# Full 128-row operands on TensorE: zero-filled low keys, padded edge tiles, and rows of rstd by transposition

## The chip, the cores and the metric

One core of a Trainium2 chip (trn2) runs the whole program in one launch. The metric is the device time of that launch in microseconds, the median of several runs. A "row" of TensorE below is a row of the contraction: the partitions over which a matmul sums. The profile writes a matmul's shape as rows\*columns of the stationary operand, then rows x columns of the moving one, so `64*128 64x256` sums over 64 partitions and moves 256 columns.

## The reference, cut to what matters

Two transformer blocks follow each other on 512 tokens of 1024 features, in float32, each of two layers. Attention heads have 64 dimensions, so a product of queries and keys sums over 64 numbers.

```
# block 1, each layer: gated MLP, three kinds of attention side by side, gated MLP
x = x + 0.5 * swiglu(rmsnorm(x), ...)
out_a = sliding_window_attn(8 heads, 2 key heads, window 128, sinks, T5 bias)
out_b = moba_attn(4 heads)             # causal softmax attention
out_c = dsa_attn(4 heads, one shared key head, the 128 best keys of each query)
x = x + concat(out_a, out_b, out_c) @ w_out
x = x + 0.5 * swiglu(rmsnorm(x), ...)
# block 2, layer 0 (even): 512 latent and 256 context tokens
q, k = rms_norm(q over 64, gain), rms_norm(k over 64, gain)    # of every head
o_a = window_attention(8 heads, latent window + context)        # with rope
o_b = neighbourhood_attention(8 heads, 8 rows x 16 columns of the grid + context)
# block 2, layer 1 (odd): latent attention, 16 heads of 64 + 32 dimensions
# both layers: residuals with gates, then a squared-ReLU MLP
```

The products run in a reduced float32 format (F32R); for accuracy each operand is split into a high part and a low part (value minus high part), and three of the four cross products are summed.

## The kernel before, in words

`Net.build` emits block 1 (`block1`: `ffn`, `mixer1`, `ffn`, twice) and block 2 (`even_mixer`, MLP, `odd_mixer`, MLP). Weights are loaded in 512 KB pieces by SP, split by ScalarE (`whi`) and VectorE (`wlo`, helper `weights`, L145 to L154), and multiplied on TensorE (`mm`, L133; `mm3`, L136). Nearly all matmuls therefore stand on L134, and VectorE's subtractions of a high part on L143 (`lo`). The framework sets an instruction order on each engine by the program's order and its own estimates; the kernel interleaves streams by generators (`weave`, `slots`, `pipeline`), so that projections or output products stand between the steps of attention. Each engine works its list in order. PSUM banks are named rings: in the attention stages "mm" has 3 banks, "s" (scores) 2, "pt" (transposed probabilities) 2, "o" 1.

**Scores of block 1** (`mixer1`). A head's query tile holds its high part on 64 partitions and its low part on the other 64; the key tile `a` holds the high part of the keys twice. One 128-row product gives high x high plus low x high. The third term, high x low, is a second product on 64 rows: the low keys of two heads lie on the two halves of one tile `l`, and `dot` (L552) multiplies the slice `half(e)` of queries and of `l`. `keys` (L532) makes these tiles: four copies on ScalarE and one subtraction on VectorE. Heads A and B take this form: per layer 4 tiles of queries x 8 heads, and 4 x 4, 48 products on 64 rows. Heads C share one key head that stands on both halves (`shared`), and take 128 rows in both products.

**Neighbourhood heads of block 2** (heads B of `even_mixer`, L1342 on). `prepare(h)` makes `qs` (queries, high and low), `ks` (keys, high twice) and `kl`, whose low part fills 64 partitions only. `attend(h, t)` has three stages, skewed by a unit each: `s1` scores (`dot`), bias and minimum on VectorE, exponential on ScalarE; `s2` transposes the probabilities to `pt`, copied to `ptb`; `s3` multiplies with the values `vb`. The tiles 0 and 3 see 192 latent keys, cut as 64 + 128, so one of their blocks has 64 rows. There are 8 heads x 6 tiles; tiles 0 to 3 have two `dot` calls, tiles 4 and 5 one: 80 in all, each of one product on 128 and one on 64 rows.

**Rows of rstd.** A norm over features sums over partitions, so its result comes with tokens on partitions and must become a row. Two helpers do that. `rstd_rows` (L203) spreads a column over 128 columns and multiplies it with the identity in float32, one product for each 128 tokens; 68 such columns in the program. `head_rows` (L1028), for two heads at once, transposes four columns (high and low of both, made by two small operations of VectorE in `head_stats`) to a tile `rows` of 4 partitions, copied by ScalarE; then a product with the constant `c_E` spreads these 4 rows to 128 partitions. It serves 13 chunks of queries and keys in `even_mixer` (`qk`: stages `evac`, `stats`, `rows`, `final`, `rotate`), the denominators of heads A (`finish_a`), the rope keys and the denominators of `odd_mixer` (`finish`): 44 products on 4 rows. For heads B the latent tokens are kept column by column of the grid (`colmajor`), and 8 of these products read `rows` in that order.

Of the kernel before, what the change touches and what calls it, by code (L numbers as in the profile page):

```python
# [17 lines left out]
T = 512  # L18
# [15 lines left out]
# column offsets of the packed per-feature vectors  # L34
# [15 lines left out]
for _n, _w in (("cos", 512), ("sin", 512), ("perm", 128), ("J", 128), ("mask_a", 640), ("mask_b", 640), ("E", 128),  # L50
               ("ones", 8), ("rt", 256), ("kr", 768), ("m2", 128)):
    CCOL[_n] = (NCST, _w)
    NCST += _w


def constants():
    """Tables that depend on shapes alone."""
# [35 lines left out]
    put("E", (np.arange(4)[:, None] % 2 == (p // 64)[None, :]).astype(np.float32))  # L93
# [9 lines left out]
    # of each token tile: cosines, then sines as they stand before the rotation of the keys' dimensions  # L103
# [10 lines left out]
class Stream:  # L114
    """tokens [c0, c0 + m) of a residual tile [128, 8, ..] and the modulation that they take"""
# [10 lines left out]
class Net:  # L126
# [51 lines left out]
    def rsqrt(self, y, v, w):  # L178
        """y = v ** -0.5 on a small tile, in float32; w is scratch of y's shape."""
# [11 lines left out]
    def rstd_y(self, acc, nt, dim, tag="mm"):  # L191
        """acc [128, nt*128]: partial sums of squares over partitions.  Returns y [128 token, nt]."""
# [27 lines left out]
    def consts(self, es):  # L220
# [5 lines left out]
        # the table of functions is loaded while the first operands come in  # L226
# [5 lines left out]
        self.c_E = cp.tile([4, 128], F32R, name="E4")  # L232
        with tc.tile_pool(name="set", bufs=1, side="right", reuse_waits="tile") as sp:
# [4 lines left out]
            nc.vector.tensor_copy(self.c_E, self.cst("E", sp, rows=4))  # L238
# [3 lines left out]
    def bias_tables(self):  # L242
        """T5 biases of heads A (window) and B, C (causal) as [query, head, key] tiles, negated; 1e30 where masked."""
# [38 lines left out]
    def pipeline(self, units):  # L282
        """Emit the stages of each unit skewed by one step; yields after every stage."""
# [27 lines left out]
    def weave(self, main, n, fill, total):  # L311
        """Emit main (n yields) with the fill (total yields) spread evenly in between."""
# [8 lines left out]
    def push(self, d, g):  # L321
        """Split chunk d of the residual, scaled by the gain in column g, for the sublayer that follows."""
# [110 lines left out]
    def pv(self, o_ps, blocks, vs):  # L433
        """o_ps [128, 64] = sum over blocks of P^T blocks (stationary) and V blocks (moving)."""
# [3 lines left out]
    def o_norm(self, o_ps, rden, nh):  # L438
        o = self.op.tile([128, 512], F32, name="o", bufs=2)
# [5 lines left out]
    def o_out(self, o, nh, dst, cols):  # L445
        """transpose o [128, nh * 64] and split it into dst = (hi, lo) [128, nh/2, tokens]."""
# [9 lines left out]
    def mixer1(self, l, nxt):  # L456
        nc, tc = self.nc, self.tc
        win, wo = self.ins["win"], self.ins["wo"]
        with ExitStack() as es:
# [7 lines left out]
            def proj(b, dst, scale=1.0):  # L467
                """one 128-column block of h @ w_in, transposed, into the tile or function dst; yields four times."""
# [37 lines left out]
            # Of two heads e on the halves of the partitions: queries [high; low] and [low; high], keys [high; high] of  # L506
            # each and the low parts as they stand
            def half(e):
                return slice(64 * e, 64 * e + 64)
# [4 lines left out]
            def ring_k(dt=F32R):  # L514
                return new("k", T, dt=dt, bufs=10)
# [16 lines left out]
            def keys(dst):  # L532
                def f(t):
                    a, b, l = [ring_k() for _ in range(3)]
                    nc.scalar.copy(a, t)
                    self.lo(l, t, a)
# [3 lines left out]
                    dst.extend([[(a, slice(0, 128)), (l, half(0))], [(b, slice(0, 128)), (l, half(1))]])  # L540
                return f

            def shared(dst):
                """keys that all heads take, on both halves already"""
                def f(t):
# [3 lines left out]
                    dst.extend([(a, slice(0, 128)), (l, slice(0, 128))])  # L549
# [20 lines left out]
            # token-major columns: va 128, vb 256, widx 4  # L570
# [15 lines left out]
            # C selects keys: scores of the index heads, then the 128 largest of each row  # L586
# [34 lines left out]
            def attn(i, heads, ob_, nh, sink, dst):  # L621
                """units of one query tile; heads: (q, k, n, bias, selection, [v blocks], sink) in order."""
# [70 lines left out]
            # phase 1: index scores between the projections of A  # L693
# [14 lines left out]
            # phase 2: A between the projections of B  # L708
# [70 lines left out]
            def fill3():  # L779
# [11 lines left out]
                t = new("t", T, bufs=2)  # L791
# [34 lines left out]
    def adaln(self):  # L826
        """generator over (layer, 128-feature block): mod[:, layer, block, cond] = silu(cond) @ ada_w."""
# [19 lines left out]
    def finish_mod(self):  # L847
# [4 lines left out]
        # gain * (1 + scale): [128, layer, sublayer, cond, chunk]  # L852
# [9 lines left out]
    def square_acc(self, s, d):  # L862
        """s.acc += squares of chunk d"""
# [9 lines left out]
    def modulate(self, s, l, sub, ma=None):  # L873
        """s.xs: split chunks of norm(x) * (1 + scale) + shift; one chunk for each step"""
# [16 lines left out]
    def normalise(self, s, l, sub, delay, gap):  # L891
        """statistics, rows of rstd and modulation of a stream, step by step"""
# [9 lines left out]
    def lin(self, w, xss, ps):  # L902
        """ps[j] [128, m] += w @ xss[j]; one step for each chunk"""
# [8 lines left out]
    def gate(self, l, k, d, s, p):  # L912
        """chunk d of the residual += gate * p"""
# [1214 lines left out]
```

## Time and profile before

| | |
|---|---|
| median of 3 runs | 3787.88 us (3785.65 to 3790.46) |
| the profiled execution: span, first to last instruction | 3790.3 us |
| PE busy | 3710.3 us (98%), 18814 matmuls |
| VectorE, ScalarE, GpSimd busy | 2246.8, 1496.8, 150.6 us |
| mean granted clock of TensorE | 0.981 of full speed |

The span is all that the profile records of its execution; it stands 2.4 us (0.06%) over the median. A matmul's record reaches from its start to the modelled end of its pipeline, so records overlap and "busy" says little; what a matmul takes from the next one is the distance from its start to the next start. A merged line of the timeline shows the first start of several equal matmuls.

### The profile page before, as it was taken

The page shows a single profiled execution, that of the slowest core. Times are in us where ns is not written, and L with a number is a line of the kernel's source. Part 1 is how long each engine was busy: PE and PEld are TensorE (multiplying, and loading weights), DVE is VectorE, ACT ScalarE, POOL GpSimd, SP SyncE. Part 2 cuts the span into 40 slices and gives each one's busy share as a digit, 9 for nine tenths or more (in the row PEclk, how much of TensorE's full clock was granted, in tenths as well). Part 3 has the DMA queues.
Part 4 walks back from the last instruction along what each step waited for, and adds up shares of the span by engine and source line. Part 5 has one row for each costly group of instructions (what it writes and reads, how often), then busy time and mean ns, then how long its engine had stood idle before and what let it go on. Part 6 is the DMA issues. An engine that isn't in the chain of part 4 may idle for free. (4 is left out here: it accounts for less than half of the span.)

```text
span 3790.3 us, 47958 instructions
## 1 busy us (share of the span) xinstructions
PE 3710.3 (98%) x18814; PEld 3093.8 (82%) x18814; DVE 2246.8 (59%) x4205; ACT 1496.8 (39%) x2580; POOL 150.6 (4%) x150
## 2 busy tenths in 40 slices
PE   8999999999999999999999999999999989999999
PEld 6888887888888887888887887778888877888887
DVE  6576675767576657654456675463333468876443
ACT  4223554322322246442234554441221347764222
POOL 1000002000000000100000000000000100100000
PEclk9999999999999999999999998899999999999999
DMA  6454212445454432133331011022112310013332
GB/s 221 127 165 144 81 57 84 156 156 167 128 168 149 141 115 63 51 116 95 100 102 59 29 49 50 17 73 67 62 62 62 90 63 24 23 52 105 99 96 95
DMA packets 115482, 356.53 MB, mean 94 GB/s; under 512 B 12468, under 2 KB 23096, under 8 KB 114744
## 3 DMA queue, kind: packets, MB, share of 16 engines
q1 hardware_dynamic: 106432, 341.32, 28.4%
q10 hardware_dynamic: 8824, 12.15, 1.1%
q8 instruction: 147, 2.41, 0.3%
q14 instruction: 79, 0.65, 0.1%
HBM read 340.85 MB, written 12.58 MB: 93 GB/s over the span
## 5 line engine op out<-in xcount | busy, mean ns | idle before, releaser
L134 PE MATMUL mm<-xs,whi 128*128 128x512 f32 (+1 forms) x3840 | 1193.3, 392 | 15.1 <-ACT whi L150 9.0
L150 ACT CAST whi<-wraw 128x1024 fp32r<-128x1024 f32 (+3 forms) x528 | 542.1, 1028 | 1603.7 <-PE mm L134 1290.1
L134 PEld LDWEIGHTS mm<-xs,whi 128*128 128x128 f32 x3840 | 718.9, 189 | 166.7 <-ACT whi L150 11.1
L134 PE MATMUL mm<-h,whi 128*128 128x512 f32 (+1 forms) x2944 | 822.2, 372 | 2.0 <-ACT whi L150 2.0
L143 DVE TENSOR_TENSOR wlo<-wraw,whi 128x1024 fp32r<-128x1024 f32 (+3 forms) x528 | 630.4, 1194 | 309.3 <-ACT whi L150 299.5
L134 PE MATMUL mm<-xs,wlo 128*128 128x512 f32 (+1 forms) x1920 | 750.3, 391 | 5.5 <-DVE wlo L143 5.2
L134 PEld LDWEIGHTS mm<-h,whi 128*128 128x128 f32 x2944 | 536.0, 188 | 108.9 <-ACT whi L150 2.2
L134 PE MATMUL mm<-h,wlo 128*128 128x512 f32 (+1 forms) x1472 | 515.9, 372 | 1.2 <-DVE wlo L143 1.2
L134 PEld LDWEIGHTS mm<-xs,wlo 128*128 128x128 f32 x1920 | 363.4, 189 | 85.3 <-DVE wlo L143 11.0
L134 PE MATMUL mm<-xslat,whi 128*128 128x512 f32 x1024 | 344.0, 413 | 11.1 <-ACT whi L150 3.6
L134 PEld LDWEIGHTS mm<-h,wlo 128*128 128x128 f32 x1472 | 264.5, 189 | 41.4 <-DVE wlo L143 1.6
L835 DVE CUSTOM_DVE_ANT_0 junk<-wraw,silu_c 128x1024 f32<-128x1024 f32 x192 | 234.5, 1221 | 97.3 <-DMA wraw<-in_ada_w 94.6
L914 DVE SCALAR_TENSOR_TENSOR x<-mm,mod,x 128x512 f32<-128x512 f32 (+1 forms) x96 | 67.7, 706 | 295.2 <-PE mm L134 295.2
L134 PEld LDWEIGHTS mm<-xsctx,whi 128*128 128x128 f32 x944 | 175.5, 193 | 41.3 <-ACT w L1105 2.9
L134 PEld LDWEIGHTS mm<-xslat,whi 128*128 128x128 f32 x1024 | 170.1, 194 | 47.0 <-DVE xslat L888 5.4
L134 PE MATMUL mm<-xslat,wlo 128*128 128x512 f32 x512 | 208.0, 407 | 0.5 <-DVE wlo L143 0.5
L134 PE MATMUL mm<-xsctx,whi 128*128 128x256 f32 x944 | 195.1, 289 | 0.1
L343 DVE SCALAR_TENSOR_TENSOR x<-mm,x 128x512 f32<-128x512 f32 x144 | 99.2, 689 | 129.9 <-PE mm L134 129.5
L397 DVE TENSOR_TENSOR t<-mm,R 128x512 f32<-128x512 f32 x88 | 60.8, 691 | 138.6 <-PE mm L134 138.1
L395 DVE TENSOR_TENSOR t<-mm,R 128x512 f32<-128x512 f32 x88 | 60.7, 689 | 135.4 <-PE mm L134 135.4
L134 PE MATMUL mm<-xsctx,wlo 128*128 128x256 f32 x472 | 134.2, 285 | 0.0
L134 PEld LDWEIGHTS mm<-xslat,wlo 128*128 128x128 f32 x512 | 99.1, 194 | 7.5 <-DVE wlo L143 1.4
(405 smaller groups left out, 4739.2 us busy)
## 6 DMA issues: line engine op xcount, KB each, us to landing
wraw<-in_gu SPq DMA_DIRECT2D x176, 512.0 KB, 3.6
wraw<-in_mlp_w SPq DMA_DIRECT2D x136, 512.0 KB, 3.5
wraw<-in_ada_w SPq DMA_DIRECT2D x96, 512.0 KB, 3.6
wraw<-in_dn SPq DMA_DIRECT2D x64, 512.0 KB, 3.7
wraw<-in_win SPq DMA_DIRECT2D x30, 512.0 KB, 3.5
wraw<-in_dn SPq DMA_DIRECT2D x32, 384.0 KB, 3.2
wraw<-in_ewin SPq DMA_DIRECT2D x18, 512.0 KB, 3.4
wraw<-in_wo SPq DMA_DIRECT2D x16, 512.0 KB, 3.6
```

The costliest lines, as they stand in the source:

```text
L134: self.nc.tensor.matmul(ps, lhsT, rhs, start=start, stop=stop)
L143: self.nc.vector.tensor_tensor(out, x, hi.bitcast(F32), op=OP.subtract)
L150: nc.scalar.copy(hi, raw)
L343: self.nc.vector.scalar_tensor_tensor(self.x[:, d, :], ps, scale, self.x[:, d, :], op0=OP.mult, op1=OP.add)
L395: nc.vector.tensor_mul(zg, ps[0], R)
L397: nc.vector.tensor_mul(zu, ps[1], R)
L835: nc.vector.tensor_tensor_reduce(j, w, self.silu_c[:, c, :], 1.0, 0.0, op0=OP.mult, op1=OP.add, accum_out=self.mod[:, l, f, c:c + 1])
L914: self.nc.vector.scalar_tensor_tensor(s.chunk(d), p, self.mod[:, l, k + d, s.cond:s.cond + 1], s.chunk(d), op0=OP.mult, op1=OP.add)
```

## The change

All products of queries and keys take 128 rows. In `mixer1` each head gets a low tile of its own (`la`, `lb`), whose other half GpSimd sets to zero; `keys` subtracts in two halves. In `prepare`, GpSimd zeroes the other half of `kl`. In `attend` the context stands first, the latent keys behind it, and the edge tiles are padded: the last 64 columns of `s` are zeroed, and `vb` has blocks for keys 0 to 127 and 128 to 255, so every block has 128 rows. `rstd_rows` transposes the spread column and no longer multiplies. `spread` (new) copies each of two columns 64 times on ScalarE, `head_rows` transposes that tile straight to PSUM, and VectorE multiplies from there; `c_E`, the high and low columns, `rows` and the stage `rows` go. To make room, `t` in `mixer1` and the tiles `o` and `sh` have one buffer where they had two; the ring `k` has 13 where it had 10. Comments go as well.

```diff
 def rstd_rows(self, y, nt, tag="mm"):
-                self.mm(pr[:, j * 128:(j + 1) * 128], y[:, j0 + j:j0 + j + 1].to_broadcast([128, 128]), self.ident,
-                        True, True)
+                self.nc.tensor.transpose(pr[:, j * 128:(j + 1) * 128], y[:, j0 + j:j0 + j + 1].to_broadcast([128, 128]),
+                                         self.ident)
...
 # mixer1
-                t = new("t", T, bufs=2) if f else dst
+                t = new("t", T) if f else dst
...
-                return new("k", T, dt=dt, bufs=10)
+                return new("k", T, dt=dt, bufs=13)
...
 def keys(dst):
-                    a, b, l = [ring_k() for _ in range(3)]
+                    a, b, la, lb = [ring_k() for _ in range(4)]
+                    nc.gpsimd.memset(la[64:].bitcast(F32), 0.0)
+                    nc.gpsimd.memset(lb[:64].bitcast(F32), 0.0)
                     nc.scalar.copy(a, t)
-                    self.lo(l, t, a)
+                    self.lo(la[:64], t[:64], a[:64])
+                    self.lo(lb[64:], t[64:], a[64:])
...
-                    dst.extend([[(a, slice(0, 128)), (l, half(0))], [(b, slice(0, 128)), (l, half(1))]])
+                    dst.extend([(a, la), (b, lb)])
...
 def dot(o, q, k, q0, k0, k1):
-                for i, (t, r) in enumerate(k):
-                    self.mm(o, q[r, q0:q0 + 128], t[r, k0:k1], i == 0, i == len(k) - 1)
+                for i, t in enumerate(k):
+                    self.mm(o, q[:, q0:q0 + 128], t[:, k0:k1], i == 0, i == len(k) - 1)
...
 def head_stats(self, sq, ones, nt, qscale, tag="mm"):
-        ys = self.sm.tile([128, nt, 4], F32R, name="ys%d" % nt)
-        y3 = y.rearrange("p (j c) -> p j c", c=2)
-        nc.vector.tensor_scalar(ys[:, :, 0:2], y3, qscale, None, op0=OP.mult)
-        nc.vector.scalar_tensor_tensor(ys[:, :, 2:4], y3, qscale, ys[:, :, 0:2].bitcast(F32),
-                                       op0=OP.mult, op1=OP.subtract)
-        return ys
+        if qscale != 1.0:
+            nc.vector.tensor_scalar(y, y, qscale, None, op0=OP.mult)
+        return y
...
+    def spread(self, y, nt):
+        t = self.rowp.tile([128, nt * 128], F32, name="spread")
+        self.nc.scalar.copy(t.rearrange("p (c d) -> p c d", d=64), y[:, :, None].to_broadcast([128, 2 * nt, 64]))
+        return t
+    def head_rows(self, t, c0, c1, tag="mm"):
+        p = self.psum(tag)
+        for j in range(c0, c1, 128):
+            self.nc.tensor.transpose(p[:, j - c0:j - c0 + 128], t[:, j:j + 128], self.ident)
+        return p[:, :c1 - c0]
...
 # even_mixer, qk: final
-                        p = self.psum()
-                        r = st["rows"][:, c0:c1]
+                        p, d = self.head_rows(st["y"], c0, c1), st["d"][:, c0:c1]
                         if colmajor and c0 == 0:
-                            r = r.rearrange("p (r c) -> p c r", r=8)
-                            self.mm(p[:, :c1 - c0].rearrange("p (c r) -> p c r", r=8), self.c_E, r, True, True)
-                        else:
-                            self.mm(p[:, :c1 - c0], self.c_E, r, True, True)
-                        nc.vector.tensor_mul(st["d"][:, c0:c1], st["d"][:, c0:c1], p[:, :c1 - c0])
+                            d = d.rearrange("p (c r) -> p c r", r=8)
+                            p = p.rearrange("p (r c) -> p c r", r=8)
+                        nc.vector.tensor_mul(d, d, p)
...
-                return proj(b, [evac, stats, rows, final] + ([rotate, lambda st: dst(st["d"])] if keep else []))
+                return proj(b, [evac, stats, final] + ([rotate, lambda st: dst(st["d"])] if keep else []))
...
 # even_mixer, heads B
+                nc.gpsimd.memset(l[o].bitcast(F32), 0.0)
                 self.lo(l[r], kb[r, c], k[r])
...
-            values = [[(0, 64, 5), (64, 128, 0)], [(0, 128, 0), (128, 128, 1)], [(0, 128, 1), (128, 128, 2)],
-                      [(128, 64, 6), (0, 128, 2)], [], []]
+            values = [[5, 7], [0, 1], [1, 2], [2, 6], [], []]
...
-                        self.mm(o, q[half(e), t * 128:(t + 1) * 128], l[half(e), k0:k1], False, True)
+                        self.mm(o, q[:, t * 128:(t + 1) * 128], l[:, k0:k1], False, True)
+                    if nl % 128:
+                        nc.gpsimd.memset(s[:, n:], 0.0)
+                    dot(p[:, :256], T, TT)
...
 # odd_mixer
 def finish(c, job):
-                ys = new(gp, "ys", 4, 4, dt=F32R, bufs=2)
-                d3 = den.rearrange("p (i h) -> p i h", h=2)
-                nc.vector.tensor_copy(ys[:, :, 0:2], d3)
-                nc.vector.tensor_tensor(ys[:, :, 2:4], d3, ys[:, :, 0:2].bitcast(F32), op=OP.subtract)
+                rows = self.spread(den, 4)
                 yield
-                rows = self.head_rows(ys, 4)
-                yield
-                p = self.psum()
-                self.mm(p, self.c_E, rows, True, True)
-                nc.vector.tensor_mul(of[:, c, :], of[:, c, :], p)
+                nc.vector.tensor_mul(of[:, c, :], of[:, c, :], self.head_rows(rows, 0, T))
```

Because stages fall away and estimates differ, the order on the engines moves too. On TensorE, in heads B of block 2, a stretch between two output products stood so before (`ks` high keys, `kl` low keys, `pt` transposed probabilities, `o` product with the values; the size is that of the output):

```order
L1147 MATMUL pt<-ident,s 64x128
L1147 MATMUL pt<-ident,s 128x128 x3
L134 MATMUL o<-vb,ptb 128x64 x4
L134 MATMUL s<-ks,qs 128x256
L134 MATMUL s<-kl,qs 128x256
L1147 MATMUL pt<-ident,s 128x128 x2
L134 MATMUL o<-vb,ptb 128x64 x4
```

The same stretch now:

```order
L1136 MATMUL pt<-ident,s 128x128 x4
L133 MATMUL o<-vb,ptb 128x64 x4
L133 MATMUL s<-ks,qs 128x256
L133 MATMUL s<-kl,qs 128x256
L1136 MATMUL pt<-ident,s 128x128 x2
L133 MATMUL o<-vb,ptb 128x64 x4
```

The number of instructions is the same; the block of 64 keys has become one of 128, and each product on `kl` still follows its partner on `ks`.

On TensorE, in the projections of `even_mixer`, the first chunk of keys took its two 4-row products here before (`rows,E`; the six transpositions of `ys` stood some thirty products ahead):

```order
L134 MATMUL mm<-xsctx,wlo 128x256
L134 MATMUL mm<-rows,E_69 128x512
L134 MATMUL mm<-xsctx,whi 128x256 x2
L134 MATMUL mm<-xsctx,wlo 128x256
L134 MATMUL mm<-xslat,whi 128x512 x2
L134 MATMUL mm<-xsctx,whi 128x256
L134 MATMUL mm<-rows,E_69 128x256
```

In their place now:

```order
L133 MATMUL mm<-xsctx,wlo 128x256
L1032 MATMUL mm<-ident,spread 128x128 x4
L133 MATMUL mm<-xslat,whi 128x512 x2
L133 MATMUL mm<-xsctx,whi 128x256 x2
L133 MATMUL mm<-xslat,wlo 128x512
L1032 MATMUL mm<-ident,spread 128x128 x2
```

The six transpositions, of 128 columns where they had 4, have come to the place of the two products on 4 rows.

On ScalarE, in the same projections, two copies of `rows` stood between the evacuations (`kb`, `w`) and the split of the next weights before:

```order
L1037 CAST rows<-mm 4x512
L1037 CAST rows<-mm 4x256
L150 CAST whi<-wraw 128x1024
L1104 ACTIVATE kb<-mm,vecs 128x512
L1104 ACTIVATE kb<-mm,vecs 128x256
```

Now one copy, which waits for VectorE's `hy`, stands there:

```order
L1024 COPY spread<-hy 128x768
L149 CAST whi<-wraw 128x1024
L1024 COPY spread<-hy 128x768
L1099 ACTIVATE kb<-mm,vecs 128x512
L1100 ACTIVATE w_16059<-mm 128x512
```

Two copies have become one, one step earlier, ahead of TensorE's transposition instead of behind it.

## Rows read from the trace of the kernel before

**Rows 1.** The page: span, and busy time of TensorE with its share.

```profile
span 3790.3 us, 47958 instructions
PE 3710.3 (98%) x18814; PEld 3093.8 (82%) x18814; DVE 2246.8 (59%) x4205; ACT 1496.8 (39%) x2580; POOL 150.6 (4%) x150
```

**Rows 2.** Timeline of TensorE, heads B of block 2: start, us, form, count.

```profile
2332.16 0.38 PE L134 MATMUL s<-kl,qs 64*128 64x256 f32 x1
2332.47 0.38 PE L134 MATMUL s<-ks,qs 128*128 128x256 f32 x1
2332.79 0.38 PE L134 MATMUL s<-kl,qs 64*128 64x256 f32 x1
2333.10 0.66 PE L1147 MATMUL pt<-ident,s 128*128 128x128 f32 x4
2333.69 1.24 PE L134 MATMUL o<-vb,ptb 64*128 64x64 f32 x8
2334.77 0.83 PE L1147 MATMUL pt<-ident,o 128*128 128x128 f32 x6
```

**Rows 3.** Groups of TensorE by form: count, busy us, mean ns; 64-row scores.

```profile
L134 PE MATMUL s<-kl,qs 64*128 64x256 f32 x64 | 26.8, 422 | 0.0
L134 PE MATMUL s<-k,x 64*128 64x256 f32 x48 | 18.3, 382 | 0.0
...
L134 PE MATMUL s<-k,q 64*128 64x128 f32 x8 | 2.6, 323 | 0.0
```

**Rows 4.** Timeline of TensorE, projections of `even_mixer`.

```profile
2040.83 0.28 PE L134 MATMUL mm<-xsctx,wlo 128*128 128x256 f32 x1
2041.03 0.49 PE L134 MATMUL mm<-rows,E 4*128 4x512 f32 x1
2041.45 0.73 PE L134 MATMUL mm<-xslat,whi 128*128 128x512 f32 x2
2042.02 0.39 PE L134 MATMUL mm<-xsctx,whi 128*128 128x256 f32 x2
2042.25 0.40 PE L134 MATMUL mm<-xslat,wlo 128*128 128x512 f32 x1
```

**Rows 5.** Groups of TensorE by form: the 4-row products, the spread columns of rstd.

```profile
L134 PE MATMUL mm<-ident,y 128*128 128x128 f32 x120 | 18.8, 302 | 8.5 <-DVE y L186 8.5
...
L134 PE MATMUL mm<-rows,E 4*128 4x512 f32 x22 | 13.1, 597 | 0.0
```

**Rows 6.** Timeline of TensorE: four spread columns in the first MLP.

```profile
38.64 0.62 PE L134 MATMUL mm<-xs,whi 128*128 128x512 f32 x2
39.10 0.39 PE L134 MATMUL mm<-xs,wlo 128*128 128x512 f32 x1
39.32 1.05 PE L134 MATMUL mm<-ident,y 128*128 128x128 f32 x8
40.13 0.71 PE L134 MATMUL mm<-xs,whi 128*128 128x512 f32 x2
```

**Rows 7.** Windows: length, busy us (count) by engine, granted clock, DMA share, GB/s.

```profile
447.00:566.00 119.00, 118.90 (x599) 93.94 (x598) 89.97 (x280) 72.00 (x178) 0.00 (x0) 0.90 0.18 59
1430.00:1549.00 119.00, 118.71 (x596) 94.06 (x596) 89.45 (x278) 71.26 (x178) 0.00 (x0) 0.90 0.19 59
2284.00:2448.00 164.00, 163.62 (x840) 128.41 (x840) 80.97 (x240) 78.04 (x177) 0.00 (x0) 0.85 0.08 21
2018.00:2268.00 250.00, 244.92 (x1543) 201.64 (x1543) 164.85 (x468) 130.62 (x283) 0.00 (x0) 1.00 0.10 32
3140.00:3390.00 250.00, 237.47 (x1536) 206.21 (x1537) 214.84 (x431) 187.30 (x400) 22.67 (x49) 0.97 0.07 21
```

**Rows 8.** Groups by form of VectorE, GpSimd and ScalarE: nearest to what is added.

```profile
L143 DVE TENSOR_TENSOR k<-t,k 128x512 fp32r<-128x512 f32 x3 | 2.0, 681 | 0.0
...
L253 POOL MEMSET v<- 128x1024 f32 x2 | 1.9, 956 | 23.1 <-DMA scr<-v 23.1
...
L1767 ACT ACTIVATE s<-s,mx 128x768 f32<-128x768 f32 x64 | 58.1, 907 | 7.8 <-DVE mx L1766 7.4
```

More of the change, by code (lines that the diff above doesn't have):

```diff
@@ L49 @@
 NCST = 0
-for _n, _w in (("cos", 512), ("sin", 512), ("perm", 128), ("J", 128), ("mask_a", 640), ("mask_b", 640), ("E", 128),
+for _n, _w in (("cos", 512), ("sin", 512), ("perm", 128), ("J", 128), ("mask_a", 640), ("mask_b", 640),
                ("ones", 8), ("rt", 256), ("kr", 768), ("m2", 128)):
@@ L1019, in head_stats @@
         self.rsqrt(y, v, w)
-        ys = self.sm.tile([128, nt, 4], F32R, name="ys%d" % nt)
-        y3 = y.rearrange("p (j c) -> p j c", c=2)
-        nc.vector.tensor_scalar(ys[:, :, 0:2], y3, qscale, None, op0=OP.mult)
-        nc.vector.scalar_tensor_tensor(ys[:, :, 2:4], y3, qscale, ys[:, :, 0:2].bitcast(F32),
-                                       op0=OP.mult, op1=OP.subtract)
-        return ys
-    def head_rows(self, ys, nt, tag="mm"):
-        nc = self.nc
-        rows = self.rowp.tile([4, nt * 128], F32R, name="rows")
-        for j0 in range(0, nt, 4):
-            k = min(4, nt - j0)
-            pr = self.psum(tag)
-            for j in range(k):
-                nc.tensor.transpose(pr[:4, j * 128:(j + 1) * 128], ys[:, j0 + j, :].bitcast(F32), self.ident)
-            nc.scalar.copy(rows[:, j0 * 128:(j0 + k) * 128], pr[:4, :k * 128])
-        return rows
+        if qscale != 1.0:
[10 more added lines that the diff above has]
+        return p[:, :c1 - c0]
     def cst(self, name, pool, rows=128):
@@ L1108, in stats @@
                 def stats(st):
[L1109 to L1112 removed]
+                    st["y"] = self.spread(self.head_stats(st["sq"], self.c_ones[:, 0:2], 6, qscale), 6)
                 def final(st):
                     for c0, c1 in self.bands(TT):
[L1116 to L1117 removed]
+                        p, d = self.head_rows(st["y"], c0, c1), st["d"][:, c0:c1]
                         if colmajor and c0 == 0:
[L1119 to L1123 removed]
+                            d = d.rearrange("p (c r) -> p c r", r=8)
+                            p = p.rearrange("p (r c) -> p c r", r=8)
+                        nc.vector.tensor_mul(d, d, p)
                 def rotate(st):
@@ L1184, in vb_t @@
                 p = self.psum("pt")
-                tr(p[:, 0:128], t[:, 640:768])
-                tr(p[:64, 128:256], t[:, 0:64])
-                tr(p[:64, 256:384], t[:, 448:512])
-                nc.scalar.copy(vb[:, 4, c], p[:, 0:128])
-                nc.vector.tensor_copy(vb[:64, 5:7, c], p[:64, 128:384].rearrange("p (a b) -> p a b", b=128))
+                for j, s in enumerate((640, 0, 448, 128)):
+                    tr(p[:, j * 128:(j + 1) * 128], t[:, s:s + 128])
+                nc.scalar.copy(vb[:, 4:8, c], p.rearrange("p (a b) -> p a b", b=128))
             va_u = vproj(0, va_t)
@@ L1282, in finish_a @@
                 nc.vector.reciprocal(den, den)
-                ys = new(pa, "ys", 6, 4, dt=F32R, bufs=2)
-                d3 = den.rearrange("p (i h) -> p i h", h=2)
-                nc.vector.tensor_copy(ys[:, :, 0:2], d3)
-                nc.vector.tensor_tensor(ys[:, :, 2:4], d3, ys[:, :, 0:2].bitcast(F32), op=OP.subtract)
-                yield
-                rows = self.head_rows(ys, 6, "pt")
+                rows = self.spread(den, 6)
                 yield
                 for c0, c1 in self.bands(TT):
-                    p = self.psum("pt")[:, :c1 - c0]
-                    self.mm(p, self.c_E, rows[:, c0:c1], True, True)
+                    p = self.head_rows(rows, c0, c1, "pt")
                     nc.vector.tensor_mul(oa[:, c, c0:c1], oa[:, c, c0:c1], p)
-                yield
+                    yield
             def attention_a(c, after):
@@ L1433, in s2 @@
                     p = self.psum("pt")
-                    for k, (c0, w, v) in enumerate(blocks):
-                        tr(p[:w, k * 128:(k + 1) * 128], u["s"][:, c0:c0 + w])
-                    full = [k for k, b in enumerate(blocks) if b[1] == 128]
-                    f0, f1 = full[0], full[-1] + 1
-                    nc.scalar.copy(ptb[:, f0 * 128:f1 * 128], p[:, f0 * 128:f1 * 128])
-                    if f0:
-                        nc.vector.tensor_copy(ptb[:64, :128], p[:64, :128])
+                    for k in range(len(blocks)):
+                        tr(p[:, k * 128:(k + 1) * 128], u["s"][:, k * 128:(k + 1) * 128])
+                    nc.scalar.copy(ptb[:, :128 * len(blocks)], p[:, :128 * len(blocks)])
                 def s3():
@@ L1445, in s3 @@
                     o = st[e]["o"]
-                    for k, (c0, w, v) in enumerate(blocks):
-                        self.mm(o[:, t * 64:(t + 1) * 64], u["pt"][:w, k * 128:(k + 1) * 128], vb[:w, v, h * 64:h * 64 + 64],
+                    for k, v in enumerate(blocks):
+                        self.mm(o[:, t * 64:(t + 1) * 64], u["pt"][:, k * 128:(k + 1) * 128], vb[:, v, h * 64:h * 64 + 64],
                                 k == 0, k == len(blocks) - 1)
@@ L1562, in odd_mixer @@
         ykv = self.rstd_y(acc["kv"], 6, 256)
-        ykr = self.head_stats(sq, self.c_ones[:, 6:8], 6, 1.0)
+        ykr = self.spread(self.head_stats(sq, self.c_ones[:, 6:8], 6, 1.0), 6)
         evac(0, "q", proj(0, (lat,)))
@@ L1566, in odd_mixer @@
         evac(1, "q", proj(1, (lat,)))
-        rows = self.head_rows(ykr, 6)
         evac(2, "q", proj(2, (lat,)))
@@ L1709, in odd_mixer @@
         for c0, c1 in self.bands(TT):
-            p = self.psum()
-            self.mm(p[:, :c1 - c0], self.c_E, rows[:, c0:c1], True, True)
-            nc.vector.tensor_mul(t[:, c0:c1], t[:, c0:c1], p[:, :c1 - c0])
+            nc.vector.tensor_mul(t[:, c0:c1], t[:, c0:c1], self.head_rows(ykr, c0, c1))
         v = kv(0)
```

33 lines of the change are left out of this document (9 added, 24 removed).

## The prediction, made before the changed kernel was timed

> **What bounds the kernel.** I read the page first: TensorE has a matmul in flight for 3710.3 of 3790.3 us [rows 1]. The reader is to see two things: no other engine comes near, and so whatever shortens TensorE's own list shortens the kernel, as long as operands arrive in time. But "busy" is no measure of use, so the second view is the timeline of TensorE, read from start to start. Plain products set the scale: two of 256 columns take 0.23 us, 0.115 each [rows 4], two of 512 columns 0.46, 0.23 each [rows 6]. In heads B of block 2 the same 256 columns take 0.31 us, whether on 64 rows or on the 128 rows between them: starts at 2332.16, 2332.47, 2332.79, 2333.10 [rows 2]. The product on 4 rows shows where it is lost: the 256-column product ahead of it takes 0.20 and not 0.115, it takes 0.42 itself and not 0.23, and the two of 512 behind it 0.57 and not 0.46 [rows 4]. So going from 128 rows to fewer costs some 0.09 + 0.19 us, and going back 0.1, beside the products themselves: about 0.39 for a visit. The third view, windows by stage, tells what each stage could give: all engines' work, and the granted clock [rows 7].
>
> **The change, part by part.** Durations are of the profiled execution, whose span of 3790.3 us stands 2.4 us over the median of the runs.
>
> *Low products on 128 rows.* There are 176: 80 on `kl`, and 96 in block 1, which the groups by form confirm ([rows 3]: first, second and last of eight groups, 176 in all). A product gets no longer by its rows, since 0.115 is the step on 128 rows. Between two score products a visit of 0.39 us goes; where transpositions follow, the way back costs less (four take 0.59 to the next start, of which four plain ones at 0.11 are 0.44, and 0.09 is already the next visit's entry [rows 2]). I take 0.37. 176 x 0.37 = **65 us**, all on TensorE's list.
>
> *Products on 4 rows.* All 44 go, with their visits: 18 of 512 columns at 0.42 + 0.20, 18 of 256 at 0.12 + 0.39, and the 8 that read by columns of the grid: the 22 records of the group of 512 columns average 597 ns [rows 5], 14 of them last 490 [rows 4], so the 8 last 0.78, which is 0.71 from start to start, and 0.20 for the visit's ends. 11.2 + 9.2 + 7.3 = **27 us**, rounded down. The transpositions ahead of them keep their number, and 128 columns are taken at the same 0.11.
>
> *Edge tiles.* Eight passes of `o`, two of them on 64 rows, take 1.08 us [rows 2]; plain ones take 0.11 each, and 0.09 goes ahead of them. 16 x 0.27 = **4 us**.
>
> *Columns of rstd.* Four columns are eight passes, 0.81 us [rows 6]; four transpositions are 0.44. With 136 passes (120 in [rows 5], 16 more on "pt") there are 17 such fours: 17 x 0.4 = **7 us**, most of it in stages where TensorE waits for nothing.
>
> *The clock.* Three stages run at a granted clock of 0.90, 0.90 and 0.85 [rows 7]. Between the levels 1.2 and 2.4 GHz that is 20, 20 and 30% of their time at the lower one: 24 + 24 + 49 = 97 us, which at 2.4 GHz would be 48 less. Before it fell, TensorE was in exactly these visits. Bounds are 0 and 48; no row shows these stages without visits, but the window with as many transpositions and none of the 64-row products, heads A of block 2, has 1.00 [rows 7]. I take half, **24 us**, since each of these stages also begins with waits that remain.
>
> *What is given back.* In the two attention stages of block 1 TensorE would be left with 119 - 48 x 0.37 - 6 (its part of the clock) = 95 us, while VectorE has 90 us of work there [rows 7] and gets two more subtractions of 0.68 us [rows 8]. No stage here runs VectorE above 86% (214.84 of 250 [rows 7]); at 90% the stage takes 101, so 6.5 us for each: **-13 us**. Heads B come to 164 - 30 - 4 - 12 = 118 us with VectorE at 81 and ScalarE at 78: two thirds, no charge. Heads A with their projections lose some 21 of 250 and keep VectorE at 72%: none.
>
> *At nothing.* GpSimd's zeroes: 12 of 64x512, 8 of 64x768, 16 of 128x64, each under the 0.96 us of 1024 columns [rows 8]; GpSimd is idle in these stages [rows 7], and the tiles have two or more buffers, so they are written a unit ahead. If all of them were waited for, it would be some 15 us. The copy to `spread`: 768 columns, at most 0.91 us [rows 8] in place of two; behind it on ScalarE stand evacuations, for whose banks TensorE waits, but at least 4 us of products lie between the statistics and the transposition. The single buffer of `t`: the next projection's evacuation waits on VectorE for four copies on ScalarE, under 3 us, and a projection of 24 products of 0.23 lies between (5.5 us); if that cover were gone, `topk` and the scores' minimum are what queues behind it. VectorE's multiplication that reads PSUM in another order: as long as before.
>
> Sum: 65 + 27 + 4 + 7 + 24 - 13 = **114 us**. 3790.3 - 114 = 3676; against the median, **3674 us**. The whole 97 us at 2.4 GHz and nothing given back would be 151, 3637; only the first four terms, and the stages of block 1 stopped at VectorE's 80% (114 us, 13 worse each) with 12 us of zeroes waited for, 65, 3723.
>
> **A rule that speaks against it.** The rows say that a short product is paid like a visit of 0.39 us. The Trainium skill, "TensorE: Matmul & The Clock Gate", Part 3 (Packing small matmuls), holds that products on different row groups run side by side, a few ns apart, so that short ones should be kept and packed; by that rule the first term would be 0, which is rival 3 below, with its time and its chance. Here a 128-row product stands between any two short ones, and none of the starts [rows 2] are closer than 0.31 us.
>
> **Rivals.**
> 1. *The other engines become the bound.* Scores, minimum, exponential, transposition, copy and product form a chain; heads B have 48 units, and the time of one falls from 3.4 to 2.4 us. For it: VectorE at 76% in block 1 already [rows 7]. Against it: the stages are skewed by a unit. With block 1 at 110 and heads B at 130 us, and 12 more of waits in heads A, the gain is 75: 3713 us.
> 2. *The clock stays at 2.4 GHz.* For it: it falls only where the visits are densest. 24 more than the forecast and part of the 13: 3642 us.
> 3. *Filling up gains nothing.* If the low product took 0.31 us because its operands alternate with the high one's, or if short products ran beside their neighbours, the visits would not be the price, and only the 4-row products and the columns of rstd would go: 34 us, 3754. Against it: products on 4 rows with other operands show the same ends [rows 4].
> 4. *Slower: the clock falls.* Shorter products leave TensorE waiting on VectorE, and more of the 538 us (652 - 114) of these four stages runs at 1.2 GHz. A microsecond of work costs one more there; without the clock's term the gain is 90, and 48 us of work is at 1.2 GHz now, so the kernel is slower when more than 138 of the 538, a quarter, are there. With a third, 179, it is 41 slower: 3829 us. For it: the three stages that are at the lower level for up to 30%. Against it: with the visits gone the products stand closer, and heads A have 1.00 with 250 us of the same kind of work [rows 7]. The same page of the Trainium skill, Part 4 (PE-mode transpose), says that transpositions do not count as work for the clock; more products become transpositions here. By it this rival would hold, but heads A, full of transpositions, contradict it.
>
> **How the numbers follow.** Forecast 57%, rival 1 16%, rival 2 20%, rival 3 3%, rival 4 4%. A difference under 0.2% cannot be told from none here. Forecast and rivals 1 to 3 are all faster by more, 95% with 1% set aside for no change; slower is 4%. From 3632 to 3722 the range takes in the forecast with both bounds of the clock, and most of rivals 1 and 2.
>
> **What would show it.** Right: score products of 256 columns 0.12 us apart; no record with 64 or 4 rows; heads B in about 118 us, each attention stage of block 1 in about 101 with VectorE at 90%; eight passes of `ident,y` become four. The clock's windows at 0.95 or more. Wrong: score products still 0.3 apart (rival 3); TensorE's idle time in these stages grown past 30 us, released by VectorE or ScalarE (rival 1); a granted clock under 0.75 there (rival 4); waits on `k` or `kl` for GpSimd, which I have at nothing.

## The result, and the profile after

The changed kernel takes 3659.78 us (median of 4 runs, 3658.88 to 3660.74) against 3786.77 us before (4 runs, 3783.89 to 3790.46): a ratio of 0.9664, 95% interval 0.965 to 0.9677. The forecast was 3674 us. The profiled execution of the changed kernel has a span of 3658.7 us, 131.6 less than that of [rows 1].

The page of the changed kernel:

```profile
span 3658.7 us, 47782 instructions
...
PE 3576.8 (98%) x18706; PEld 3036.4 (83%) x18706; DVE 2235.9 (61%) x4146; ACT 1492.9 (41%) x2562; POOL 165.9 (5%) x186
```

TensorE's share is 98% as before, with 108 fewer matmuls and 133 us fewer: over the whole span the bound has not moved to another engine. Two pairs of score products, behind products with the values (`o`) and ahead of an output product, stood so in TensorE's timeline in heads B before:

```profile
2310.28 0.36 PE L134 MATMUL s<-ks,qs 128*128 128x256 f32 x1
2310.57 0.38 PE L134 MATMUL s<-kl,qs 64*128 64x256 f32 x1
2310.88 0.39 PE L134 MATMUL s<-ks,qs 128*128 128x256 f32 x1
2311.20 0.38 PE L134 MATMUL s<-kl,qs 64*128 64x256 f32 x1
2311.51 0.50 PE L134 MATMUL mm<-xslat,wlo 128*128 128x512 f32 x1
```

Such a unit now reads:

```profile
2253.00 0.58 PE L133 MATMUL o<-vb,ptb 128*128 128x64 f32 x4
2253.39 0.36 PE L133 MATMUL s<-ks,qs 128*128 128x256 f32 x1
2253.59 0.28 PE L133 MATMUL s<-kl,qs 128*128 128x256 f32 x1
2253.71 0.28 PE L133 MATMUL s<-ks,qs 128*128 128x256 f32 x1
2253.82 0.28 PE L133 MATMUL s<-kl,qs 128*128 128x256 f32 x1
2253.94 0.63 PE L133 MATMUL mm<-xslat,whi 128*128 128x512 f32 x2
```

Three of the four score products are 0.11 to 0.12 us from the next start; they were 0.31 and 0.32. The first, behind products of 64 columns, takes 0.20 where it took 0.29. All four take 0.55 us where they took 1.23. The windows by stage (columns as in [rows 7], the same five stages):

```profile
446.00:546.00 100.00, 97.87 (x612) 85.69 (x610) 91.58 (x286) 72.32 (x181) 0.00 (x0) 0.97 0.22 70
1404.00:1505.00 101.00, 98.65 (x616) 86.98 (x616) 93.00 (x289) 73.17 (x182) 0.64 (x1) 0.97 0.21 70
2209.00:2322.00 113.00, 112.09 (x835) 102.94 (x834) 76.13 (x225) 77.42 (x174) 6.50 (x21) 0.99 0.13 36
1970.00:2196.00 226.00, 223.64 (x1514) 197.69 (x1513) 157.72 (x444) 127.19 (x265) 0.74 (x1) 1.00 0.10 35
3010.00:3243.00 233.00, 221.64 (x1416) 194.46 (x1417) 200.31 (x397) 177.70 (x382) 21.46 (x48) 0.96 0.06 19
```

The attention stages of block 1 went from 119 to 100 and 101 us, heads B from 164 to 113, heads A with their projections from 250 to 226, the odd layer's heads from 250 only to 233 (a stretch cut a little wider before; between the same two products it is 230.9 and 230.3). The granted clock rose where it had been lowest: 0.90, 0.90 and 0.85 became 0.97, 0.97 and 0.99. In the odd layer's heads it did not rise (0.97 and 0.96). Marked off by the same products in both timelines, the 131.6 us come from these places (each figure rounded by itself):

| stretch | before | after | less |
|---|---|---|---|
| block 1, layer 1, first to last score product | 194.3 | 172.8 | 21.5 |
| block 1, layer 2, the same | 194.7 | 172.7 | 22.0 |
| end of block 1's heads C to the last score product of heads A | 667.4 | 642.6 | 24.9 |
| heads B, first to last score product | 159.0 | 108.6 | 50.4 |
| all else (the whole is the difference of the spans) | | | 12.8 |

### The profile page after: what moved, and what is told of

It is laid out like the page before. It is cut to its first block, busy times and chain, and to the rows that moved or that the text cites. A ratio compares the mean times of both kernels' runs of the same rounds, so it can differ in the third digit from the quotient of the medians.

```text
span 3658.7 us, 47782 instructions
## 1 busy us (share of the span) xinstructions
PE 3576.8 (98%) x18706; PEld 3036.4 (83%) x18706; DVE 2235.9 (61%) x4146; ACT 1492.9 (41%) x2562; POOL 165.9 (5%) x186
## 4 chain that ended last, share of the span: by engine, by line
PE 89%; DVE 6%; ACT 3%; issue 1%; DMA 1%; ACTq 0%; SPq 0%; DVEq 0%
PE mm L133 77%; PE o L133 4%; PE s L133 4%; PE pt L1136 1%; DVE wlo L142 1%; PE mm L1749 1%; PE pt L662 1%; PE pt L133 1%; DVE xs L325 0%; ACT whi L149 0%; DVE u L883 0%; DVE xslat L885 0%; PE mm L1032 0%; DVE m L610 0%; ACT s L1743 0%
## 5 line engine op out<-in xcount | busy, mean ns | idle before, releaser
L133 PE MATMUL mm<-xs,whi 128*128 128x512 f32 (+1 forms) x3840 | 1189.7, 391 | 11.8 <-ACT whi L149 8.5
L133 PE MATMUL mm<-xslat,whi 128*128 128x512 f32 x1024 | 333.7, 403 | 6.6 <-DVE xslat L885 2.6
```

The source lines that it names most:

```text
L133: self.nc.tensor.matmul(ps, lhsT, rhs, start=start, stop=stop)
```

## Experiments

The theory: what the change removes is the price of going to fewer rows and back, some 0.39 us a visit, and with the visits the time at the lower clock. The rivals: the price hangs on each short product, filling up gains nothing, VectorE limits block 1, and the clock follows something else.

### One part alone: low keys of heads B

The kernel before with this alone (a2_kl):

```diff
+                nc.gpsimd.memset(l[o].bitcast(F32), 0.0)
                 self.lo(l[r], kb[r, c], k[r])
...
-                        self.mm(o, q[half(e), t * 128:(t + 1) * 128], l[half(e), k0:k1], False, True)
+                        self.mm(o, q[:, t * 128:(t + 1) * 128], l[:, k0:k1], False, True)
```

> The kernel before with one part of the change: only the low keys of heads B (80 products) on 128 rows; low products of block 1, 4-row products and edge tiles as before. Visits are the price (V): 80 x 0.37 = 30 us go, and with the visits half of heads B's lower clock, 12 us: 42 us, 3745 us; score products of heads B 0.12 us apart, granted clock of heads B near 0.93. Rival N, filling up gains nothing: within 5 us of 3787, products still 0.31 apart. Rival C, the clock stays up as soon as the low visits are gone, though the edge tiles' visits remain: 30 + 24 = 54 us, 3733 us, clock of heads B at 0.98 or more.

3749.04 us, ratio 0.99 (0.9885 to 0.9914), 33 to 44 us less. Heads B, in the windows of this kernel:

```profile
2282.00:2396.00 114.00, 113.68 (x810) 102.23 (x811) 77.23 (x237) 73.94 (x168) 4.39 (x6) 0.98 0.09 24
```

The size is theory V's, the clock rival C's: 0.98, although the edge tiles' visits remain. Both can't hold with 0.37 for a visit; what a visit is worth is taken up in the account below. From first to last score product heads B last 113.8 us, 45 less than in the profile before. A second profile of the kernel before, shown below, has 146.7 us there; against that it is 33. The padded edge tiles take 5 more, their bit of the clock included (113.8 to 108.6), where 4 were forecast.

### One part undone: low keys of heads B, low keys of block 1

The changed kernel with the diff above reversed (c1_kl64):

> The changed kernel with the low keys of heads B back on 64 rows, their edge tiles still padded. V: 80 x 0.37 = 30 us and half of heads B's clock, 12: 3660 + 42 = 3702 us. Rival C, the whole of the lower clock comes with the visits: 30 + 24 = 54, 3714 us, granted clock of heads B at 0.87 or less. Rival: the edge tiles' visits were what brought the clock down: 30 us, 3690, clock at 0.97 or more.

3698.77 us, ratio to before 0.9757 (0.9742 to 0.9771): 39 us over the 3659.78 of the changed kernel, and 35 by the ratios, each of which is taken against runs of the kernel before beside it. V has 42, and the rival that blames the edge tiles 30. The clock speaks against that rival: heads B show 0.90 (below), and not 0.97 or more. The changed kernel with `la` and `lb` taken back into one `l`, as in the part of the diff on `mixer1`, reversed, and with 10 buffers for `k` (d1_low64):

> The changed kernel with the low keys of block 1 (96 products) back on 64 rows, all else as changed. V: 96 x 0.37 = 36 us come back; in the two attention stages of block 1 (48 of the 96) the clock falls to about 0.90 again, 12 us, less what VectorE was said to take there (13): 3660 + 35 = 3695 us. Rival C, the clock is worth the whole of its lower stretches: 24 us and no VectorE limit: 3660 + 60 = 3720 us. Rival N: within 5 us of 3660.

3708.77 us, ratio 0.9791 (0.9775 to 0.9808): 49 us over the changed kernel (48 by the ratios), between V's 35 and rival C's 60. From first to last score product the stages of block 1 last 193.2 and 193.8 us, 20.4 and 21.1 longer. That is 41.5 of the 49; of the rest 4.4 us lie between heads B and the odd layer's heads, where this execution has 10.6 us more at the lower clock. Windows of d1_low64 over these stretches, and then of the changed kernel:

```profile
417.00:610.00 193.00, 191.61 (x998) 155.33 (x998) 142.81 (x401) 113.42 (x265) 13.06 (x12) 0.95 0.19 60
1396.00:1590.00 194.00, 192.98 (x1001) 156.84 (x1000) 143.29 (x401) 113.48 (x265) 13.07 (x12) 0.94 0.18 60
```

```profile
414.00:587.00 173.00, 169.96 (x1001) 147.29 (x1000) 144.00 (x404) 113.38 (x266) 13.92 (x12) 0.98 0.21 68
1373.00:1545.00 172.00, 168.74 (x997) 146.82 (x996) 143.70 (x403) 112.95 (x264) 13.94 (x12) 0.98 0.21 68
```

VectorE's and ScalarE's work is the same; TensorE's grew, and the clock fell. Of 20.4 us, 48 visits at 0.37 are 17.8, and the time at the lower clock (20.5 us in the first stage against 6.8) is worth half of the difference, 7. Together that is 4 us too many. TensorE's idle time in these windows accounts for some 1.7 of it (3.0 us in the changed kernel, 1.4 here); the rest is a visit worth less than 0.37, or waits too short to show. Filling up is what gains: rival N falls here, and in a2_kl too.

### Columns of rstd alone; products on 4 rows and edge tiles alone

The kernel before with `rstd_rows` transposing (a4_R):

> The kernel before with only the columns of rstd by transposition. Four columns take 0.44 in place of 0.81 us; 17 fours x 0.4 = 7 us: 3780 us, eight passes on ident,y become four. Rival: the statistics are waited for anyway, so that the time goes into a wait: 0 us, 3787.

3780.43 us, ratio 0.9977 (0.9968 to 0.9986): 5 to 12 us less, 7 forecast. The group of [rows 5] in this kernel:

```profile
L210 PE MATMUL mm<-ident,y 128*128 128x128 f32 x60 | 11.1, 308 | 8.6 <-DVE y L186 8.6
```

Half the passes, and the wait for VectorE ahead of them as long as it was (8.5): the time saved did not turn into a wait.

The changed kernel with all low products on 64 rows again and the columns of rstd as products (a3_rows):

> The kernel before with the 44 products on 4 rows replaced by transposed spread columns and the edge tiles padded (single buffers too); all 176 low products on 64 rows and the columns of rstd as before. V: 27 + 4 = 31 us and a little of the clock in heads B (2 to 6): 3752 us. Rival: the products on 4 rows were hidden or their place is taken by waits on the copy to spread: under 10 us, 3777 or more. Rival C: the lower clock needs the edge tiles' visits as well as the low ones: 31 + 20 = 51 us, 3736.

3742.69 us, ratio 0.9888 (0.9873 to 0.9903): 37 to 48 us less, above V's 31 and towards rival C. From the end of block 1's heads C to the last score product of heads A it takes 643.8 us, 23.7 less than before and close to the 24.9 of the whole change; that is the products on 4 rows, which were not hidden (32 of the 44 stand in this stretch). What exceeds 31 is the clock in heads B, where all 80 low products are on 64 rows and the stage still lasts only 137 us:

```profile
2260.00:2397.00 137.00, 136.73 (x809) 108.83 (x808) 76.07 (x221) 76.16 (x167) 2.27 (x15) 0.98 0.09 24
```

### The clock of heads B, looked at again

c1_kl64 runs the same instructions in heads B as a3_rows, at another clock. A second profile of each (a3_look, c1_look), and of the kernel before (before_look):

> A second profile of the kernel of a3_rows. It and c1_kl64 have the same instructions in heads B (low keys on 64 rows, edge tiles padded), yet the first profiles show 6 and 30 us of that stage at the lower clock. If the clock in a stage full of visits varies from one execution to the next, this one shows another figure, anywhere from 5 to 45 us, and heads B last 137 to 160 us by it. If it hangs on what the kernel does before heads B (the columns of rstd, block 1), it shows 6 again, within 3 us.

> A second profile of the kernel of c1_kl64. Varying from one execution to the next: another figure than 30 us at the lower clock in heads B, 5 to 45. Hanging on what comes before: 30 again, within 3 us.

> A second profile of the kernel before. Varying: the lower clock in heads B is not 49.5 us again but anywhere from 25 to 60. Fixed by the code: 49.5 again, within 3 us.

The spans are 3739.1, 3700.2 and 3779.3 us. Heads B in c1_kl64 and in c1_look:

```profile
2211.00:2358.00 147.00, 146.88 (x809) 116.84 (x809) 75.53 (x221) 75.94 (x168) 2.28 (x15) 0.90 0.08 22
```

```profile
2213.00:2360.00 147.00, 146.88 (x809) 116.97 (x808) 75.70 (x221) 75.97 (x168) 2.29 (x15) 0.90 0.09 23
```

And in before_look:

```profile
2285.00:2432.00 147.00, 147.00 (x810) 115.09 (x811) 78.93 (x237) 74.92 (x169) 0.00 (x0) 0.93 0.08 21
```

Each of the two experiments repeats itself between first and last score product: c1_kl64 with 29.6 and 29.4 us at the lower clock, a3_rows with 6.2 and 6.8. The kernel before does not: 49.5 in the first profile and 21.5 here, with heads B at 159.0 and 146.7 us from first to last score product. That is 12.3 us, about the whole distance between the two spans (11.0). So neither expectation holds throughout. The 28.0 us more at the lower clock cost 12.3, or 0.44 for each, a little under the half that I count. Two more runs do not touch heads B, a4_R (above) and b3_bufs (below), and their profiles show 39.9 and 35.2 us. Where the low products take 128 rows there is far less: 4.4 us in a2_kl, 0.2 in the changed kernel, 0.8 to 2.5 in d1_low64, e1_topk and b2_zero3. Block 1 is steadier. Each of its stages has 20.5 to 23.9 us at the lower clock in every profile with its low products on 64 rows, and 3.4 to 6.8 in every one without.

With visits in them, heads B run at the lower clock for 6 to 50 us. How long depends on something that these edits don't hold, and what that is stays open. In the kernel before and in c1_kl64 the clock falls in the waits ahead of the stage (TensorE waits 4.1 us for the table `hk` in the kernel before), and then stays at 1.2 GHz for 23.9 and 27.3 us; in the changed kernel it falls there too (a wait of 3.8 us), and is back at 2.4 GHz after 3.4.

### Visits or short products?

The kernel before, with the second group's low product ahead of its high one, so that two 64-row products stand together (b1_swap):

```diff
-                        dot(p[:, off:off + n], q, k, i * 128, (i + 1) * 128 - n, (i + 1) * 128)
+                        dot(p[:, off:off + n], q, k[::-1] if g else k, i * 128, (i + 1) * 128 - n, (i + 1) * 128)
```

(`g` counts the groups of a unit; likewise in `attend`, for the second `dot`.)

> The kernel before with every product on the rows it had, but of two groups of scores in a row the second takes its low product first, so that two 64-row products stand side by side: 40 of block 1's 96 and 32 of heads B's 80 lose their own visit. Theory V, the price is the change of row count: 72 visits x 0.37 = 27 us go, and up to 10 of the clock: 3752 us; the second of two 64-row products starts 0.12 us after the first. Rival P, the price hangs on each short product, however it is placed: within 5 us of 3787, and 0.3 us between the two.

3760.06 us, ratio 0.9912 (0.9893 to 0.993): 26 to 41 us less, with every product on the rows it had. In the trace 36 pairs of block 1 and 29 of heads B stand side by side, 65 of the 72. Block 1's stages are 5.9 and 4.8 us shorter, heads B 18.5 or 6.3, by which profile of the kernel before they are held against: part of the gain is heads B's clock (28.4 us at the lower one here). What the order alone does, the timeline in heads B shows:

```profile
2310.80 0.36 PE L134 MATMUL s<-ks,qs 128*128 128x256 f32 x1
2311.10 0.50 PE L134 MATMUL s<-kl,qs 64*128 64x256 f32 x2
2311.52 0.38 PE L134 MATMUL s<-ks,qs 128*128 128x256 f32 x1
2311.74 0.63 PE L134 MATMUL mm<-xslat,whi 128*128 128x512 f32 x2
```

Two short products together take 0.42 us where one alone takes 0.31 [rows 2]: the second adds 0.11, a plain step. (The two starts lie 0.21 apart and not 0.12 as I expected, since the exit is paid in the second one.) The unit takes 0.94 us from its first start; it took 1.23 in the kernel before and takes 0.55 in the changed one. With the same two short products it is 0.29 us shorter, so the price belongs to the change of row count, and rival P falls.

### VectorE in block 1; the zeroes; the single buffers

The changed kernel with rounds of `topk` left out (e1_topk):

```diff
-                    for i in (3, 2, 1):
+                    for i in (3, 2, 1) if r % 4 == 0 else ():
```

> The changed kernel with 12 of the 16 rounds of topk in each layer left out (its selection of keys is then too small). VectorE loses some 35 of its 92 us in each attention stage of block 1 and no product changes. Theory of the prediction: VectorE keeps TensorE from about 6 us in each: 100 to 101 becomes 94 to 95, 13 us in all, 3647 us. Rival: TensorE's own list and the rest of the lower clock set these 100 us, VectorE at 92% does not: within 4 us of 3660, stages 99 to 101 us.

3663.57 us, ratio 0.9665 (0.9651 to 0.968), that of the changed kernel (0.9664). The attention stages of block 1:

```profile
448.00:548.00 100.00, 96.96 (x613) 84.87 (x612) 59.92 (x182) 72.47 (x181) 2.15 (x3) 0.98 0.20 65
1408.00:1508.00 100.00, 96.95 (x610) 84.66 (x610) 59.41 (x180) 71.90 (x181) 2.18 (x3) 0.98 0.20 65
```

VectorE has 60 us of work in place of 92, and TensorE goes through as many products in the same 100 us (172.4 us from first to last score product, 172.8 in the changed kernel). VectorE at 92% does not limit it. TensorE's waits in the first of these stages of the changed kernel, from the view of waits (who waited, for whom; us, times, longest):

```profile
PE s L133 <- ACT x L514: 0.9, 1, 0.9
PE mm L133 <- ACT t L778: 0.6, 1, 0.6
PE s L133 <- DVE nm L651: 0.5, 1, 0.5
```

The changed kernel with each zero written three times (b2_zero3):

> The changed kernel with each of GpSimd's zeroes written three times: three times their time on GpSimd. At nothing, as predicted: within 4 us of 3660. Rival, they are waited for: twice up to 15 us more, 3670 to 3690, with waits of TensorE or VectorE on k or kl for GpSimd.

3663.58 us, ratio 0.9663 (0.9649 to 0.9678), again that of the changed kernel; no wait of TensorE or VectorE names GpSimd. The zeroes of the changed kernel, from the groups of GpSimd:

```profile
L1357 POOL MEMSET kl<- 64x768 f32 x8 | 5.9, 734 | 262.1 <-ACT ph L1241 225.0 <-PE s L133 37.1
...
L529 POOL MEMSET k<- 64x512 f32 x6 | 3.1, 522 | 0.3
L530 POOL MEMSET k<- 64x512 f32 x6 | 3.1, 521 | 0.3
L1400 POOL MEMSET s<- 128x64 f32 x16 | 2.4, 151 | 122.6 <-PE pt L1136 56.3 <-ACT spread L1024 49.0 <-ACT ptb L1419 17.2
```

That is 14.5 us, hidden whole. The kernel before with `t`, `o` and `sh` in one buffer (b3_bufs):

> The kernel before with the tiles t, o and sh in one buffer in place of two, all else as before. Put at nothing in the prediction: within 4 us of 3789. Rival: the evacuation behind waits on the copies, some 0.5 to 3 us for each of 30 projections: 15 us or more, 3804.

3785.1 us, ratio 0.9998 (0.9988 to 1.0007): nothing, as put.

## Why the prediction was right, step by step

- **What bounds.** TensorE's list, before and after: it has a matmul in flight for 98% of either span. VectorE at 92% in block 1 does not limit it (e1_topk).
- **Low products, 65 us.** The mechanism is shown by b1_swap (fewer changes of row count, same products). The price of 0.37 holds where it is read from start to start: two visits ahead of an output product cost some 0.77 us in heads B (the four score products 1.23 against 0.55, the 512-column product behind them 0.33 against 0.23). By stages a visit is worth less. From a3_rows to the changed kernel heads B, both nearly always at 2.4 GHz, lose 28.3 us; with 3 of it for the clock that leaves 0.32 for each of 80. In d1_low64 the two stages of block 1 give 13.6 and 12.5 us for 48 visits each once half of the lower clock is taken off, 0.26 to 0.28. By this estimate the term is about 51 us, 14 too high, with the small waits of the shorter stages counted in.
- **Products on 4 rows, 27 us; edge tiles, 4.** The stretch with 32 of the 44 is 23.7 us shorter in a3_rows, where the forecast's prices make 20.5. But eight of the others stand in the odd layer's heads, 5.0 us by the same prices, and there the kernel gained 0.6. The time at the lower clock between the first score product and the last product with the values went from 11.8 to 18.9 us. It goes mostly with this part of the change: 9.8 to 12.9 us in the six profiles that keep the products on 4 rows, 16.6 to 18.9 in seven of the eight without them, among them the two of a3_rows, and 13.2 in b2_zero3. That was not foreseen, and why it is so stays open. The edge tiles took 5 us with their bit of the clock.
- **Columns of rstd, 7 us.** a4_R shows 5 to 12.
- **The clock, 24 us.** This term was too small. I took half of what the lower clock cost in three stages, because the waits at their start remain. They remain, but the time at the lower clock shrank to 6.8, 6.8 and 0.2 us, from 23.9, 23.9 and 49.5: 83 us, worth half, 42. The bound of 48 held the term. For heads B the 49.5 is one execution's figure: another profile has 21.5, with which it is 55 us, worth 28. The runs of the kernel before scatter over 12 to 15 us beside the experiments, those of the changed one over 2 in its four runs. The prediction's ground, that TensorE was in these visits before the clock fell, is not the whole of it: the longest stretch in heads B began in a wait.
- **Given back, 13 us.** The stages of block 1 came out at 100 and 101 us with VectorE at 92% in both, as forecast (101, 90%), and the step is wrong all the same. e1_topk takes a third of VectorE's work away there and nothing moves. TensorE's products in the first stage, each at the median step of its form at 2.4 GHz, come to 93 us. Of the 7 above them, the 6.8 us still at the lower clock are worth 3, and idle time, in waits of 0.9 us and less, on ScalarE above all, is 2.1; some 2 us are too small a piece to place.
- **Luck in the sum.** Without the clock the forecast has 103 - 13 = 90 us. With half of all time at the lower clock taken off (145.1 us in the profile before, 54.9 after) the spans differ by 86.5. The two agree because the 13 charged to VectorE stand for about what the low products were put too high. With VectorE rightly at nothing, the forecast would have been 3661 us, nearer still, by two errors that nearly cancel: the clock too low, the visits too high.
- **At nothing.** GpSimd's zeroes and the single buffers: shown by b2_zero3 and b3_bufs. The copy to `spread`: no run of its own, but a3_rows, which has it, gains no less than forecast in the stretch where most of these copies stand.
- **Sums.** Two are off by little. An edge tile is 1.08 - 0.88 + 0.09 = 0.29 us, not 0.27, and the gain of rival 1 is 114 - 18 - 12 - 12 = 72 us, not 75 (3716 us). Neither moves the range.
- **Rivals.** Rival 1 has no sign: TensorE is idle 2.1 and 2.4 us in block 1's stages, 0.9 in heads B. Rival 2 is nearest in its mechanism (the clock came back nearly whole), without its 3642 us, since the low products gave less. Rival 3 falls with c1_kl64 and d1_low64: undone alone, the low products cost 35 to 39 and 48 to 49 us. The rule beside it is the Trainium skill's, "TensorE: Matmul & The Clock Gate", Part 3 (Packing small matmuls): short products on different row groups run side by side. No run here tests it. Each short product shares rows with its 128-row neighbours, the pairs of b1_swap lie on the same half, and pairs on different halves next to each other were not tried. Rival 4: the clock is at 0.97, 0.97, 0.99 and 1.00 in the four stages that it named; a little of it shows in the odd layer, which it did not name.

## What to carry to other kernels

Read TensorE from start to start where products of different row counts alternate: here a lone 64-row product between 128-row ones costs 0.34 to 0.39 us more than a full one by the timeline, and about 0.3 by the stage, so zeros written by an idle engine pay, and where they don't fit, putting the short products next to each other saves a visit for each pair (b1_swap). Count the clock with it: a stage in which TensorE is slowed by such visits may run at 1.2 GHz for part of its time, and here got nearly all of that back (97 us in three stages became 14). Take such a figure from more than one execution. An engine at 92% in a stage is not its limit as long as TensorE hardly waits for it; take some of its work away before charging for it.

## What the runs showed of the hardware that I had not expected

- The lower clock in one and the same stage of one and the same kernel was 49.5 us in one execution and 21.5 in another, while c1_kl64 and a3_rows repeated theirs within 0.6 us. The scatter of the runs of the kernel before (3779.26 to 3794.1 us beside these experiments) is of the size of this one stage's clock; the changed kernel, with 0.2 us at the lower clock there, scattered by 2 us over four runs.
- The price of a visit does not grow with the number of short products in it: one takes 0.31 us, two side by side 0.42, and the second adds no more than the 0.11 of a plain step.
- With every product on 128 rows, time at the lower clock shrank in three stages and grew in the odd layer's heads (11.8 to 18.9 us). It grew there in a3_rows too (16.6), where the low products of queries and keys are still short.
